# Sum of squares of the context tokens in the first norm: sixteen one-column matmuls into one PSUM bank in place of seven GpSimd additions and two matmuls

## The chip, the cores and the metric

One NeuronCore of a Trainium2 chip runs the whole program in one launch. The metric is device time in microseconds (us), the median over runs. The five engines have queues of their own and meet at semaphores: TensorE (PE in the profile; its weight loads are PEld), VectorE (DVE), ScalarE (ACT), GpSimd (POOL) and SyncE (SP, which here issues nearly all transfers).

## The reference, cut to what matters

A trunk of two layers over 512 latent and 256 context tokens, 1024 features, all in fp32. Each layer normalises the tokens, modulates them, projects them, mixes and attends, and ends in a squared-ReLU MLP. Context tokens go through the same weights with a modulation of their own. The change is in the first `rmsnorm` of layer 0, for the context tokens alone.

```python
def rmsnorm(x, g):
    xf = x.astype(jnp.float32)
    y = xf * lax.rsqrt(jnp.mean(xf * xf, axis=-1, keepdims=True) + EPS)
    return (y * g.astype(jnp.float32)).astype(x.dtype)
...
for l in range(DEPTH):                               # DEPTH = 2
    m_lat = modulation(c, w_mod[l], b_mod[l])        # silu(c) @ w_mod + b_mod: shifts, scales, gates
    m_ctx = modulation(c_ctx, w_mod[l], b_mod[l])
    h_lat = rmsnorm(x_lat, norm1_g[l]) * (1 + sc1) + sh1
    h_ctx = rmsnorm(x_ctx, norm1_g[l]) * (1 + csc1) + csh1
    z_lat, z_ctx = h_lat @ w_in[l], h_ctx @ w_in[l]  # q, k, v, u, gate
    # QK norm, rotary, attention (latents see context and latents), gated spatial mixing
    x_lat = x_lat + ga1 * (jnp.concatenate([attn_lat, gm_lat], -1) @ w_out[l])
    x_lat = x_lat + ga2 * sqrelu_mlp(modulate(rmsnorm(x_lat, norm2_g[l]), sh2, sc2), w_ff1[l], w_ff2[l])
    # the same for x_ctx in layer 0
return x_lat
```

## The kernel before

**Layout.** The stream lies transposed on the chip, features on the 128 partitions and tokens along the row. It is held in four tiles `X`, each with two blocks of 128 features by 768 tokens (512 latent, then 256 context), so there are KT = 8 feature blocks. Weights and activations are split in a rounded part `hi` and a remainder `lo`, and each product is three matmuls (hi·hi, hi·lo, lo·hi, line L203). ScalarE makes `hi` and VectorE makes `lo` (L207 and L208 for weights, L482 and L477 for normalised tokens, whose tiles are called `A`).

**The norm.** Class `Norm` does it in four steps. `step(k)` squares block k on ScalarE (L439, L442) and adds it to one tile `acc` (L444): on GpSimd for the context norm `cx`, on VectorE for the latent norm `lat`. `sums()` multiplies each 128 tokens of `acc` by a column of ones on TensorE (L453), which leaves a sum for each token on its own partition. VectorE then scales it (L456), takes the reciprocal root in nine small operations (L287 to L297) and spreads it on a diagonal, `w` (L466). `bcast()` turns that diagonal into a row on all partitions by one more matmul (L470, into a `pt` bank), and `apply()` multiplies and adds, block by block: L481 on VectorE into a tile `s`, L482 on ScalarE, L477 on VectorE.

**Shared buffers.** The squares (L442, `tsm`) and the products of `apply` (L481) come from one pool of three buffers, tag `s`. PSUM has two pairs of banks `pa`, two banks `pb`, two banks `pt`.

**The start.** `start()` is where the change lies. It loads and multiplies the modulation weights (`mod_chunk`, L338 and L351, into `pb` and `pt`), finishes the latent norm, and interleaves the first projection `kv0` (keys and values, `wide`, into two tiles `pa`). In between it places the context norm: `cx.step` for the eight blocks (`PAR['CL']` is 0), then `lat.apply` of blocks 4 to 7, then `cx.sums()` (`PAR["CS"]` is 0), then `kv0.wide` of blocks 4 and 5. After `start()` come `cx.bcast()`, `cx.apply`, the rest of `wide` and layer 0 itself: `u_part` (columns of `u`, into `pb`), `kv.bank(2)` (keys and values of the context tokens, into `pt`), and so on.

**What sets the order.** Inside `start()` TensorE and VectorE are under a manual schedule, and the framework's scheduler orders the rest; each engine then works through its queue strictly in that order. All transfers are issued by SyncE, whose order is the same in both kernels.

Of the kernel before, what the change touches and what calls it, by code (L numbers as in the profile page):

```python
# [11 lines left out]
AF = mybir.ActivationFunctionType  # L12
ALU = mybir.AluOpType
AX = mybir.AxisListType

D = 1024
KT = 8
# [5 lines left out]
EPS = 1e-6  # L23
# [137 lines left out]
def trunk(ctx: ExitStack, tc: tile.TileContext, xT, pk1, pk2, rope, wsT, w_mod, w_tok, w_u, w_out, w_ff1, w_ff2, outT):  # L161
    nc = tc.nc
    vec, act, pe, pool_e = nc.vector, nc.scalar, nc.tensor, nc.gpsimd
# [10 lines left out]
    def nm(s):  # L174
        seq[0] += 1
        return f"{s}_{seq[0]}"

    def unit(tag, shape, dt=F32R):
        return units.tile(shape, dt, tag=tag, name=nm(tag))
# [4 lines left out]
    def tsm(shape, dt=F32):  # L184
        return tmp.tile(shape, dt, tag="s", name=nm("s"), bufs=3)
# [4 lines left out]
    def small(n, dt=F32, tag="m", bufs=9):  # L190
        return tmp.tile([128, n], dt, tag=tag, name=nm(tag), bufs=bufs)
# [7 lines left out]
    def pt(shape=(128, 512)):  # L199
        return psum.tile(list(shape), F32, tag="t", name=nm("pt"), bufs=2)  # L200

    def mm(out, a, b, start, stop, n):
        pe.matmul(out, a, b, start=start, stop=stop)  # L203
        fl.vt += max(n / 2.4, 113.0) + 3.0
# [14 lines left out]
    def convert():  # L219

        if held:
            split(*held.pop(0))
# [57 lines left out]
    def rsqrt(v, n, l=0):  # L280

        if l:
            y = small(n)
            pool_e.tensor_tensor(out=y, in0=v, in1=mhalf[:, 0:n], op=ALU.pow)
            return y
        yi = small(n, I32)
        vec.tensor_scalar(yi, v.bitcast(I32), -0.5, 1595932665.0, op0=ALU.mult, op1=ALU.add)  # L287
        y = yi.bitcast(F32)
        t, r = small(n), small(n)
        vec.tensor_tensor(out=t, in0=y, in1=y, op=ALU.mult)  # L290
        vec.scalar_tensor_tensor(out=t, in0=t, scalar=-0.703952253, in1=v, op0=ALU.mult, op1=ALU.mult)
        vec.scalar_tensor_tensor(out=y, in0=t, scalar=1.681914091, in1=y, op0=ALU.add, op1=ALU.mult)
        vec.tensor_tensor(out=t, in0=y, in1=y, op=ALU.mult)
        vec.tensor_tensor(out=r, in0=t, in1=v, op=ALU.mult)
        vec.tensor_scalar(t, r, 0.375, -1.25, op0=ALU.mult, op1=ALU.add)
        vec.tensor_tensor(out=t, in0=t, in1=r, op=ALU.mult)
        vec.scalar_tensor_tensor(out=y, in0=t, scalar=1.875, in1=y, op0=ALU.add, op1=ALU.mult)  # L297
        return y
# [6 lines left out]
    ones = const.tile([128, 128], F32, name="ones")  # L305
# [3 lines left out]
    X = [unit(f"X{i}", [128, 2, T], F32) for i in range(4)]  # L309
# [17 lines left out]
    def mod_chunk(l, j, lag=1200.0):  # L327


        ps = pb()  # L330
        ns = PAR["NS"] if j < 4 else 4
        rows = ns * 32
        for kb in range(0, 4, ns // 2):
            ws_ = take("mod", l, j, kb)[:ns // 2]
            for k2 in range(ns):
                k = kb * 2 + k2
                q = k2 * 32
                pe.matmul(ps[q:q + 32, :], S32[:, k, :], ws_[k2 // 2][:, k2 % 2 * 512:(k2 % 2 + 1) * 512], start=k < ns, stop=k >= KT - ns)  # L338
            fl.vt += PAR["MV"] * ns
            if j > 3:  # L340
                release()
            if kb < 4 - ns // 2:
                yield

        tr = (tw if l == 0 and j < 4 else tsm)([128, 512])
        vec.transpose(tr[0:rows], ps[0:rows])

        def fin():
            p4 = pt((128, 4, 2))
            for a in range(4):  # L350
                pe.matmul(p4[a * 32:a * 32 + 32], P1("sel")[0:rows], tr[0:rows].rearrange("p (m a i) -> p a m i", m=4, a=4)[:, a, :, 0:2], start=True, stop=True)  # L351
            mod_store(l, j, p4)
        if lag:
            fl.defer(lag, fin)
        else:
            fin()
        yield
# [56 lines left out]
    cx = kv0 = None  # L414
# [8 lines left out]
    def run(gen):  # L423
        for _ in gen:
            fl.tick()


    class Norm:
        def __init__(self, l, w, off, n, cond):
            self.l, self.w, self.off, self.n, self.cond = l, w, off, n, cond  # L430
            self.acc = None
            self.tagn = 1 << (2 * l + w)

        def step(self, k):
            off, n = self.off, self.n
            if k == 0:
                tg = "acc0" if off == 0 else "acc1"
                self.acc = tmp.tile([128, n], F32, tag=tg, name=nm(tg), bufs=1)
                act.activation(self.acc, xk(0)[:, off:off + n], AF.Square)  # L439
                return  # L440
            sq = (tw if self is cx and PAR['SQ'] else tsm)([128, n])
            act.activation(sq, xk(k)[:, off:off + n], AF.Square)  # L442
            eng = pool_e if k < 7 and PAR["NP"] & self.tagn or self is cx else vec
            eng.tensor_tensor(out=self.acc, in0=self.acc, in1=sq, op=ALU.add)  # L444
# [624 lines left out]
    def start():  # L1069
        nonlocal held  # L1070
        for k in range(KT):
            lat.step(k)
        run(mod_chunk(0, 0, PAR["S0"]))
        lat.sums()
        run(mod_chunk(0, 2, PAR["S2"]))
        convert()
        lat.bcast()
        fl.tick(PAR["S2"])
        lat.apply(h0, range(4))
        kv0.passes(0)  # L1080
        run(mod_chunk(0, 1, PAR["S1"]))
        for k in range(KT if PAR['CL'] == 0 else 0):
            cx.step(k)
        g = mod_chunk(0, 3, 1.0)
        for k in range(4):
            next(g)
            if k == 3:
                convert()
            kv0.wide([k])
            fl.tick()  # L1090
        fl.tick(1.0)
        lat.apply(h0, range(4, KT), lambda k: convert() if k == 6 else None)
        for k in range(KT if PAR['CL'] == 1 else 0):
            cx.step(k)
        if PAR["CS"] == 0:
            cx.sums()
        kv0.wide(range(4, PAR["KB"]))
        if PAR["CS"] == 1:
            cx.sums()
# [4 lines left out]
    lat, cx = Norm(0, 0, 0, 512, 0), Norm(0, 0, 512, 256, 1)  # L1104
# [4 lines left out]
    if PAR["MS"]:  # L1109
        with tc.manual_schedule(engines=MSS[PAR["MS"]]):  # L1110
            start()
    else:
        start()
# [65 lines left out]
```

## Time and profile before

| | |
|---|---|
| median of 3 runs | 1510.93 us (1507.56 to 1514.46) |
| profiled execution | 1510.43 us, span in the trace 1508.6 us |
| busy over the span | PE 97%, PEld 85%, DVE 60%, ACT 42%, POOL 23% |
| mean granted clock of TensorE | 0.994 of full speed |
| L444 additions on POOL, in the start | 7, from 37.46 us on for 6.43 us |
| L453 for the context | 4 passes from 43.95 us on |

In the rows below, times are microseconds from the span's start. A row of the timeline has the start, the time it takes, the engine, the line, the operation, the tile it writes, an arrow and the tiles it reads, the shape, and the number merged; in square brackets stands how long the engine was idle before it and what ended that. On TensorE a row's duration includes the way through the array, so the pace of a series is read from starts. A row of the stretches has its bounds and length, then for PE, PEld, DVE, ACT and POOL the busy time and, in brackets, the instructions, then the granted clock of TensorE (1 is full), the share of the transfer engines that is busy, and GB/s.

### The profile page before, as it was taken

Reading aid. Unit: us, or ns where it says so; the run is one execution under the profiler, and the core shown is the slowest. Engines: PE = TensorE matmul, PEld = TensorE weight load, DVE = VectorE, ACT = ScalarE, POOL = GpSimd, SP = SyncE. Lnnn points to the kernel's source line nnn. Section 1 sums busy time; section 2 is a strip of 40 time slices with the busy share of each in tenths; the row PEclk is TensorE's granted clock in tenths of the full one; section 3 lists DMA queues with packets and bytes.
Section 4 is the critical chain, followed back from the end, with each engine's and each line's share of the span. In section 5 each row is a group of like instructions: output and inputs, shape, how many; then the busy total and the mean of one; then the engine's idle time right before and its main releaser. Section 6 shows DMA issues by size and latency. Waiting matters only on the chain.

```text
span 1508.6 us, 22398 instructions
## 1 busy us (share of the span) xinstructions
PE 1461.8 (97%) x8804; PEld 1289.5 (85%) x8804; DVE 908.6 (60%) x1667; ACT 641.0 (42%) x1078; POOL 342.1 (23%) x322
## 2 busy tenths in 40 slices
PE   6899899999999999999999999999999999999998
PEld 2899787797889899898989888997898888888887
DVE  5877967786755555444444537766887544444443
ACT  3543355674545353433333224536774333322221
POOL 0112421312145552322323213146222000000000
PEclk9999999999999999999999999999999999999999
DMA  9221344401133334333433211221001333333232
GB/s 363 65 71 57 112 176 162 140 1 43 60 112 126 114 124 126 103 122 111 126 112 126 98 56 57 88 81 57 29 1 56 113 98 98 98 98 98 98 95 73
DMA packets 49945, 148.80 MB, mean 99 GB/s; under 512 B 5424, under 2 KB 6832, under 8 KB 49840
## 3 DMA queue, kind: packets, MB, share of 16 engines
q1 hardware_dynamic: 49264, 146.46, 29.6%
q8 instruction: 69, 1.13, 0.3%
q10 hardware_dynamic: 576, 0.92, 0.2%
q14 instruction: 36, 0.29, 0.1%
HBM read 145.26 MB, written 2.10 MB: 98 GB/s over the span
## 4 chain that ended last, share of the span: by engine, by line
PE 83%; DVE 8%; ACT 3%; DMA 2%; POOL 2%; issue 2%; SPq 0%; POOLq 0%; ACTq 0%; DVEq 0%
PE pa L203 52%; PE pb L203 23%; PE pt L860 3%; PE pt L203 2%; PE pb L338 1%; POOL acc L444 1%; DMA raw<-in_w_tok 1%; DMA B<-in_w_mod 1%; PE pt L642 1%; DMA A<-in_w_mod 1%; DVE A L863 1%; DVE m L841 1%; DVE B L977 1%; ACT w L844 1%; PE pb L881 0%
## 5 line engine op out<-in xcount | busy, mean ns | idle before, releaser
L203 PE MATMUL pa<-A,hi 128*128 128x384 f32 (+2 forms) x1696 | 450.5, 348 | 1.9 <-ACT w L970 0.6
L207 ACT CAST hi<-raw 128x1024 fp32r<-128x1024 f32 x171 | 179.6, 1051 | 478.2 <-PE pa L203 378.1
L208 DVE TENSOR_TENSOR lo<-raw,hi 128x1024 fp32r<-128x1024 f32 x155 | 196.9, 1270 | 230.7 <-ACT hi L207 227.3
L203 PEld LDWEIGHTS pa<-A,hi 128*128 128x128 f32 x1696 | 305.5, 189 | 26.5 <-ACT w L970 1.8
L203 PE MATMUL pa<-A,lo 128*128 128x384 f32 (+2 forms) x848 | 294.1, 347 | 1.0 <-DVE lo L208 1.0
L203 PE MATMUL pa<-B,hi 128*128 128x512 f32 (+1 forms) x900 | 239.8, 355 | 3.6 <-DVE X L800 3.6
L382 POOL TENSOR_TENSOR C<-C,s 128x512 f32<-128x512 f32 x112 | 164.9, 1489 | 314.6 <-ACT s L381 272.6
L203 PEld LDWEIGHTS pa<-B,hi 128*128 128x128 f32 x900 | 158.8, 189 | 31.6 <-DVE X L800 5.9
L203 PEld LDWEIGHTS pa<-A,lo 128*128 128x128 f32 x848 | 159.8, 189 | 12.4 <-DVE lo L208 1.5
L800 DVE SCALAR_TENSOR_TENSOR X<-pa,modT,X 128x512 f32<-128x512 f32 x126 | 82.9, 660 | 140.9 <-PE pa L203 140.9
L203 PE MATMUL pb<-B,hi 128*128 128x512 f32 (+1 forms) x600 | 156.9, 350 | 0.9 <-DVE X L800 0.9
L203 PE MATMUL pa<-B,lo 128*128 128x512 f32 (+1 forms) x450 | 157.7, 355 | 0.0
L203 PE MATMUL pb<-hi,A 128*128 128x256 f32 x672 | 126.2, 285 | 0.0
L800 DVE SCALAR_TENSOR_TENSOR X<-pb,modT,X 128x512 f32<-128x512 f32 (+3 forms) x116 | 70.8, 618 | 81.8 <-PE pb L203 81.6
L203 PEld LDWEIGHTS pb<-B,hi 128*128 128x128 f32 x600 | 104.3, 189 | 16.0 <-DVE X L800 2.6
L203 PEld LDWEIGHTS pb<-hi,A 128*128 128x128 f32 x672 | 106.1, 191 | 0.3 <-PE pb L203 0.2
L203 PE MATMUL pb<-B,lo 128*128 128x512 f32 (+1 forms) x300 | 104.5, 348 | 0.0
L203 PE MATMUL pb<-lo,A 128*128 128x256 f32 x336 | 95.3, 284 | 0.0
L203 PEld LDWEIGHTS pa<-B,lo 128*128 128x128 f32 x450 | 84.1, 189 | 11.4
L381 ACT ACTIVATE s<-k,silu 128x512 f32<-128x512 f32 x112 | 76.9, 715 | 38.8 <-DMA k<-in_w_mod 25.9
L203 PE MATMUL pb<-A,hi 128*128 128x512 f32 (+2 forms) x288 | 81.7, 360 | 2.4 <-POOL A L791 2.4
L844 ACT ACTIVATE w<-pa,m 128x768 f32<-128x768 f32 (+1 forms) x80 | 65.6, 820 | 33.7 <-DVE m L841 25.2
(173 smaller groups left out, 2234.6 us busy)
## 6 DMA issues: line engine op xcount, KB each, us to landing
raw<-in_w_ff SPq DMA_DIRECT2D x128, 512.0 KB, 3.5
k<-in_w_mod SPq DMA_DIRECT2D x96, 256.0 KB, 3.0
raw<-in_w_tok SPq DMA_DIRECT2D x19, 512.0 KB, 3.4
raw<-in_w_out SPq DMA_DIRECT2D x16, 512.0 KB, 3.5
lo<-in_w_mod SPq DMA_DIRECT2D x16, 512.0 KB, 4.5
hi<-in_w_mod SPq DMA_DIRECT2D x16, 512.0 KB, 3.7
A<-in_w_mod SPq DMA_DIRECT2D x8, 512.0 KB, 9.7
raw<-in_w_u SPq DMA_DIRECT2D x8, 512.0 KB, 3.5
```

The source lines that it names most:

```text
L203: pe.matmul(out, a, b, start=start, stop=stop)
L207: act.copy(hi, src)
L208: (eng or vec).tensor_tensor(out=lo, in0=src, in1=hi.bitcast(F32), op=ALU.subtract)
L338: pe.matmul(ps[q:q + 32, :], S32[:, k, :], ws_[k2 // 2][:, k2 % 2 * 512:(k2 % 2 + 1) * 512], start=k < ns, stop=k >= KT - ns)
L381: act.activation(p, w, AF.Copy, scale=s)
L382: pool_e.tensor_tensor(out=a, in0=a, in1=p, op=ALU.add)
L444: eng.tensor_tensor(out=self.acc, in0=self.acc, in1=sq, op=ALU.add)
L642: pe.transpose(p[:, o:o + 128], stk[:, t, hh, c0:c0 + 128].bitcast(F32), ident)
L800: vec.scalar_tensor_tensor(out=xs, in0=src[:, s - off:e - off], scalar=modT[l][:, i * 8 + m, cond:cond + 1], in1=xs, op0=ALU.mult, op1=ALU ...
L841: vec.tensor_reduce(out=nmx, in_=ps[:, 0:nk], axis=AX.X, op=ALU.max, negate=True)
L844: act.activation(p, ps[:, 0:nk], AF.Exp, bias=nmx, accum_out=sm)
L860: pe.transpose(tp_[:, (kt - k0) * 128:(kt - k0) * 128 + 128], p[:, kt * 128:kt * 128 + 128], ident)
```

## The change

The eight `cx.step` calls go. In place of `cx.sums()` stands `cx.quick()`: ScalarE squares two feature blocks at once (256 tokens each, so 512 elements a partition), four times, and TensorE multiplies every 128 tokens of every block by the column of ones, all added in two columns of one `pt` bank. GpSimd has no part in it any more. The squares now stand behind `lat.apply`, ahead of `kv0.wide` of blocks 4 and 5.

```diff
+        def quick(self):
+            ps = pt()
+            nt = self.n // 128
+            for i in range(4):
+                sq = tsm([128, 2, self.n])
+                act.activation(sq, X[i][:, :, self.off:self.off + self.n], AF.Square)
+                for t in range(nt):
+                    for a in range(2):
+                        pe.matmul(ps[:, t:t + 1], sq[:, a, t * 128:(t + 1) * 128], ones[:, 0:1], start=i == 0 and t == 0 and a == 0, stop=i == 3 and t == nt - 1 and a == 1, skip_group_check=True)
+            v = small(nt)
+            vec.tensor_scalar(v, ps[:, 0:nt], 1.0 / D, EPS, op0=ALU.mult, op1=ALU.add)
+            self.diag(rsqrt(v, nt, self.l))
...
         run(mod_chunk(0, 1, PAR["S1"]))
-        for k in range(KT if PAR['CL'] == 0 else 0):
-            cx.step(k)
         g = mod_chunk(0, 3, 1.0)
...
         lat.apply(h0, range(4, KT), lambda k: convert() if k == 6 else None)
-        for k in range(KT if PAR['CL'] == 1 else 0):
-            cx.step(k)
         if PAR["CS"] == 0:
-            cx.sums()
+            cx.quick()
         kv0.wide(range(4, PAR["KB"]))
```

Three places show how the order moves. In the changed kernel the lines between the first hunk and `start()` are 14 higher, and the sums are L443.

**TensorE, behind the last modulation matmuls (L351).** `pt_408` is the bank of the sums, `pa_317` that of the projection `kv0`. Before:

```order
L351 MATMUL pt_383<-w_367,c_70 32x8 x4
L453 MATMUL pt_408<-ones,acc_74_291 128x1 x2
L203 MATMUL pa_317<-hi_134,A_43_175 128x256
L203 MATMUL pa_317<-lo_135,A_43_175 128x256
L203 MATMUL pa_317<-hi_134,A_43_175 128x256 x2
```

Now, with `pb_568` and `pb_598` the banks of two parts of `u`, whose weights are `hi_142`, `lo_143` and `hi_146`:

```order
L351 MATMUL pt_360<-w_344,c_70 32x8 x4
L203 MATMUL pb_568<-A_39_171,hi_142 128x512 x2
L203 MATMUL pb_598<-A_39_171,hi_146 128x512 x2
L203 MATMUL pb_568<-A_39_171,lo_143 128x512
L203 MATMUL pb_568<-A_40_172,hi_142 128x512 x2
L443 MATMUL pt_385<-ones,s_386 128x1 x4
L203 MATMUL pb_568<-A_40_172,lo_143 128x512
L203 MATMUL pb_568<-A_41_173,hi_142 128x512 x2
L203 MATMUL pb_568<-A_41_173,lo_143 128x512
L203 MATMUL pb_568<-A_42_174,hi_142 128x512 x2
L443 MATMUL pt_385<-ones,s_392 128x1 x4
L203 MATMUL pb_568<-A_42_174,lo_143 128x512
```

Seven matmuls of `u` stood behind the sums and now stand ahead of the first group of them; the third and the fourth group follow the last row shown, each behind two more matmuls of `u`, and then come the 24 matmuls of `kv0` on blocks 4 and 5.

**ScalarE, at the squares.** `A_43` to `A_46` are the `hi` parts of the latent blocks 4 to 7, `hi_142` and `hi_146` the casts of the two `u` weights. Before:

```order
L442 ACTIVATE s_305<-X_3_78 128x256
L442 ACTIVATE s_308<-X_4_79 128x256
L442 ACTIVATE s_311<-X_4_79 128x256
L482 ACTIVATE A_43_175<-s_390,modT_90 128x512
L207 CAST hi_142<-raw_140 128x1024
L482 ACTIVATE A_44_176<-s_393,modT_90 128x512
L207 CAST hi_146<-raw_144 128x1024
L482 ACTIVATE A_45_177<-s_397,modT_90 128x512
L482 ACTIVATE A_46_178<-s_403,modT_90 128x512
L207 CAST ws_165<-raw_163 128x512
```

Now:

```order
L496 ACTIVATE A_43_175<-s_367,modT_90 128x512
L207 CAST hi_142<-raw_140 128x1024
L496 ACTIVATE A_44_176<-s_370,modT_90 128x512
L207 CAST hi_146<-raw_144 128x1024
L496 ACTIVATE A_45_177<-s_374,modT_90 128x512
L440 ACTIVATE s_386<-X_1_76 128x512
L496 ACTIVATE A_46_178<-s_380,modT_90 128x512
L440 ACTIVATE s_392<-X_2_77 128x512
L440 ACTIVATE s_398<-X_3_78 128x512
L440 ACTIVATE s_404<-X_4_79 128x512
L207 CAST ws_165<-raw_163 128x512
```

The squares moved from ahead of the four `A` rows to between and behind them. In the built program `s_392` takes the buffer of `s_386`, and `s_404` that of `s_392`, so each of these two squares waits for the TensorE group that reads the buffer.

**TensorE, at the projection of the context tokens.** `pt_667` (now `pt_666`) is the bank of `kv.bank(2)`, `pb_637` (now `pb_636`) that of the context part of the first `u`. Before, the last of 42 matmuls into the one, and then the other:

```order
L203 MATMUL pt_667<-hi_134,A_43_175 128x256
L203 MATMUL pt_667<-hi_134,A_44_176 128x256
L203 MATMUL pt_667<-lo_135,A_44_176 128x256
L203 MATMUL pt_667<-hi_134,A_44_176 128x256
L203 MATMUL pb_637<-A_39_171,hi_142 128x256 x2
```

Now, the last of 25:

```order
L203 MATMUL pt_666<-lo_135,A_46_178 128x256
L203 MATMUL pt_666<-hi_134,A_46_178 128x256
L203 MATMUL pt_666<-hi_114,A_39_171 128x256
L203 MATMUL pb_636<-A_39_171,hi_142 128x256 x2
L203 MATMUL pb_636<-A_39_171,lo_143 128x256
```

Seventeen matmuls of that bank went behind the `u` part. Some 30 rows further on the two orders of TensorE run alike again (into `pb_768`, now `pb_767`, its second half of tokens), and from there to the end nothing differs on any engine.

## The prediction

> **What bounds the kernel.** I read the busy shares first, then who waited for whom on TensorE, then stretches of the start, then its timeline.
>
> ```profile
> PE 1461.8 (97%) x8804; PEld 1289.5 (85%) x8804; DVE 908.6 (60%) x1667; ACT 641.0 (42%) x1078; POOL 342.1 (23%) x322
> ...
> PE pb L338 <- DVE w L621: 5.6, 1, 5.6
> PE pt L453 <- POOL acc L444: 4.0, 1, 4.0
> ```
>
> TensorE is the bound. GpSimd's additions cost it one wait of 4.0 us, at the place of the change. The stretches split there (the third ends where the bank of `kv.bank(2)` begins, the fourth where the two orders become alike):
>
> ```profile
> 39.98:43.95 3.97, 0.01 (x2) 0.00 (x1) 2.23 (x6) 1.64 (x4) 3.60 (x5) 0.89 0.40 132
> 43.95:49.89 5.94, 5.94 (x27) 5.84 (x28) 5.79 (x8) 3.76 (x5) 0.00 (x0) 0.50 0.19 44
> 49.89:64.31 14.42, 14.42 (x78) 12.43 (x77) 10.90 (x35) 5.43 (x12) 0.00 (x0) 1.00 0.24 74
> ...
> 43.00:43.20 0.20, 0.00 (x0) 0.00 (x0) 0.14 (x2) 0.06 (x1) 0.12 (x2) 0.66 0.18 62
> 43.20:43.60 0.40, 0.00 (x0) 0.00 (x0) 0.40 (x1) 0.40 (x1) 0.40 (x1) 0.50 0.00 0
> ...
> 180.00:182.00 2.00, 0.76 (x8) 0.00 (x0) 2.00 (x1) 1.60 (x3) 2.00 (x2) 1.00 0.78 260
> 182.00:183.00 1.00, 0.00 (x0) 0.00 (x0) 1.00 (x2) 0.00 (x0) 1.00 (x1) 1.00 0.92 377
> 183.00:184.00 1.00, 0.00 (x0) 0.00 (x0) 1.00 (x1) 0.00 (x0) 1.00 (x1) 0.51 0.32 127
> ```
>
> The wait cost more than itself: the granted clock fell to 0.50 at 43.06 (a mean of 0.66 over 43.00 to 43.20) and stayed there until 49.89, though TensorE worked without a gap from 43.95 on. All that could be won here is the wait and half of the 5.94 us, 6.9 us.
>
> **The change on TensorE's path.** The rows that price it, from the timeline:
>
> ```profile
> 17.66 1.05 PE L453 MATMUL pt<-ones,acc 128*128 128x1 f32 x8
> 17.66 0.97 PEld L453 LDWEIGHTS pt<-ones,acc 128*128 128x128 f32 x8 [0.84 <-issue]
> 39.74 0.24 PE L351 MATMUL pt<-w,c 64*32 64x8 f32 x8
> 43.95 1.01 PE L453 MATMUL pt<-ones,acc 128*128 128x1 f32 x4 [3.96 <-POOL acc L444]
> 44.82 0.56 PE L203 MATMUL pa<-hi,A 128*128 128x256 f32 x1
> 47.96 0.63 PE L203 MATMUL pb<-A,hi 128*128 128x512 f32 x1
> 48.38 0.63 PE L203 MATMUL pa<-hi,A 128*128 128x256 f32 x2
> 55.91 0.60 PE L470 MATMUL pt<-w,ones 128*128 128x256 f32 x2
> 56.15 0.58 PE L203 MATMUL pb<-A,hi 128*128 128x512 f32 x1
> 64.31 0.28 PE L203 MATMUL pt<-hi,A 128*128 128x256 f32 x1
> 69.34 0.40 PE L203 MATMUL pb<-A,hi 128*128 128x256 f32 x2
> 78.04 0.36 PE L203 MATMUL pb<-hi,A 128*128 128x256 f32 x1
> ```
>
> The two sums of 256 tokens are four passes, so the sixteen are 32. A pass costs its weight load: 0.97 / 8 = 0.12 us at full clock, (44.82 − 43.95) / 4 = 0.22 at half. A matmul of 512 columns takes 48.38 − 47.96 = 0.42 us at half clock and (64.31 − 56.15) / 35 = 0.23 at full; one of 256 takes (69.34 − 64.31) / 42 = 0.12.
>
> When each group can start is set by ScalarE and VectorE:
>
> ```profile
> 7.60 0.61 ACT L442 ACTIVATE s<-X 128x512 f32<-128x512 f32 x1
> 43.14 0.72 ACT L482 ACTIVATE A<-s,modT 128x512 fp32r<-128x512 f32 x1 [1.22 <-DVE s L481]
> 43.77 1.03 ACT L207 CAST hi<-raw 128x1024 fp32r<-128x1024 f32 x1
> 44.71 0.72 ACT L482 ACTIVATE A<-s,modT 128x512 fp32r<-128x512 f32 x1
> ...
> 40.26 0.45 DVE L411 SCALAR_TENSOR_TENSOR A<-modT,c 128x8 f32<-128x8 f32 x1
> 42.31 1.56 DVE L481 SCALAR_TENSOR_TENSOR s<-X,A,pt 128x512 f32<-128x512 f32 x2 [1.61 <-POOL acc L444]
> 43.90 0.75 DVE L477 SCALAR_TENSOR_TENSOR A<-s,modT,A 128x512 fp32r<-128x512 f32 x1
> 44.57 0.74 DVE L481 SCALAR_TENSOR_TENSOR s<-X,A,pt 128x512 f32<-128x512 f32 x1
> 46.13 1.22 DVE L208 TENSOR_TENSOR lo<-raw,hi 128x1024 fp32r<-128x1024 f32 x1
> 50.38 0.15 DVE L456 TENSOR_SCALAR m<-pt 128x2 f32<-128x2 f32 x1
> 50.82 0.69 DVE L208 TENSOR_TENSOR ws<-raw,ws 128x512 fp32r<-128x512 f32 x1 [0.29 <-ACT ws L207]
> 53.20 0.43 DVE L466 TENSOR_TENSOR w<-c,m 128x256 f32<-128x256 f32 x1
> 56.54 0.87 DVE L481 SCALAR_TENSOR_TENSOR s<-X,A,pt 128x256 f32<-128x256 f32 x2 [2.92 <-PE pt L470]
> 67.61 0.67 DVE L696 SCALAR_TENSOR_TENSOR C<-s,pb 128x512 f32<-128x512 f32 x1
> ```
>
> *Removed.* GpSimd held `apply` too: its product L481 waited 1.61 us for a buffer `s`. It now starts at 40.71, when L411 ends, and ScalarE follows at 41.5 (product 0.74). The queue there is unchanged up to the second cast, so `hi_142` ends at 43.2 (0.63 from one start to the next, then 1.03) and, behind `A_44`, `hi_146` at 44.75 (its weights have landed: nothing moves from 43.20 to 43.60, by the last column above, and no transfer changes its place). GpSimd's seven additions and ScalarE's eight squares fall away beside other work.
>
> *The first wait that is left.* TensorE is done with L351 at 39.98 and now waits for `hi_142`: 43.22 − 39.98 = 3.24 us where it was 3.97. Two matmuls (0.85 at half clock), then 0.73 until `hi_146` at 44.80, two more, then 0.14 for `lo_143`. VectorE makes that from 44.5 on, behind two products and two `lo` parts, and needs 1.22. Three more matmuls end at 47.07.
>
> *The groups.* `s_386` follows `A_45` on ScalarE and is ready at 45.9, so no wait. Its eight passes at half clock take 1.74 us, to 48.8. Then `s_392` may be written (0.61, to 49.6), while six matmuls of `u` run: at half clock until 49.89, if the clock keeps its times, then at full, to 50.70. The second group ends at 51.67, two matmuls at 52.13, the third group at 53.1; `s_404`, which could start at 51.8, is there at 52.4. The cast of `ws` moves behind it and ends at 53.0, ahead of VectorE's L208 on it, which stands behind L456. Two matmuls and the fourth group end at 54.53. The exchange between the two engines is thus covered, by 1.1 us in each case; without that cover each of two squares would cost up to 0.6.
>
> *Behind the groups.* `kv0` on blocks 4 and 5 (24 matmuls, 2.88 us) ends at 57.4. VectorE's chain takes 53.63 − 50.38 − 0.29 = 2.96 us from L456 to the diagonal, so the diagonal comes at 57.6. Before, it was done long ahead of L470 (53.63 against 55.91). Now TensorE waits 0.25 us for it. L470 (0.24), 24 matmuls for blocks 6 and 7, 9 and 22 of 512 for `u` (7.2) lead to the `kv.bank(2)` matmuls at 68.0, which began at 64.31 before. Twenty-five of them (3.0) lead to `pb_636` at 71.0. Its bank must be free: L696 ended at 68.28 in a chain that L470 started and that was dense from 56.54 on; L470 comes 1.75 later, so it ends at 70.0, a second before it is needed. From there 78.04 − 69.34 = 8.70 us, and seventeen matmuls (2.04), to the point where the orders meet: 81.75 against 78.04.
>
> **The sum**, by TensorE's time up to that point: waits 3.24 + 0.73 + 0.14 + 0.25 − 3.97 = +0.4; passes 1.74 + 24 × 0.12 − 0.87 = +3.8; half clock −0.5 (4.1 us of matmuls at half instead of 5.07, half of each lost). Together **+3.7 us**. Beyond that point the engines work in the same order, and the delay reaches the end, as these rows say:
>
> ```profile
> 120.00:130.00 10.00, 10.00 (x86) 10.00 (x86) 5.67 (x24) 1.84 (x4) 1.67 (x2) 1.00 0.06 22
> 130.00:180.00 50.00, 49.59 (x417) 47.95 (x419) 46.03 (x139) 19.39 (x32) 15.94 (x12) 1.00 0.25 86
> ```
>
> TensorE is full there and VectorE idle for 4.3 of 10 us, waiting for matmuls.
>
> The unknown cost is a pass placed between long matmuls. The nearest rows have them in a row. Were its load wholly hidden behind the matmul ahead, the passes would cost nothing and the sum would be about 0; were each to take the half-clock price throughout, 28 × 0.22 gives +6.2 for that term and some 6 in all. I take 0.12, since eight in a row at full clock is just what a group is. Against the profiled execution of 1510.43 us the sum gives 1514.1; the median of the runs shown lies 0.5 above that execution, so 1514.6.
>
> **Rivals.** *The clock stays at full speed* (0.2). The Trainium skill, "TensorE: Matmul & The Clock Gate", section "What's actually happening", has the clock return to half after at least one idle window of about 3.4 us. By that the wait of 3.24 us would leave it at full. The trace speaks against a full window of idleness as the condition: here the clock fell at 183.0 and at 43.06 after less.
>
> By the rows, at 183.0 it fell after some 2.2 us without a matmul (0.76 us of work in 180 to 182), at 43.06 after 3.1. A wait of 3.24 us lies near enough to both that it may or may not. If it doesn't fall, the groups end at 52.66 and L470 starts at 55.8 instead of 57.65: 1.9 less, so +1.8 us, 1512.7.
>
> *The clock stays at half through the groups* (0.12, the side of slower). It stayed at half in 43.06 to 46.5 with TensorE busy for 2.5 of 3.4 us, so it wants more than that; if passes of one column don't count as work, every stretch with a group in it falls short until the last is through. Then the second group ends at 53.1 and the fourth at 58.3, L470 starts at 62.0 instead of 57.65, 4.3 later: +8.0 us, 1518.9. It decides from the point where the clock still reads 0.50 at 56; one stretch more alone gives +5.3.
>
> *The delay is absorbed* (0.08). At 186 TensorE waits 5.6 us for VectorE (L621, above). If VectorE's queue there came from work that doesn't follow TensorE, that wait would swallow all: 1510.9. Its idle time at 120 to 130 speaks against it.
>
> **How the numbers follow.** My path has 0.55, the three rivals 0.4, and 0.05 is left for what I don't see, spread to both sides. The runs of before differ by 6.9 us, so 0.5% (7.6 us) is about what can be told from no change. The range reaches from the absorbed delay, less a microsecond of that spread, to the slow clock: 1510 to 1519.5. Only the slow clock and the spread above my path reach 1518.5: slower 0.13. Faster by 0.5% would need more than the 6.9 us that could be won, at no cost: 0.04. Same: 0.83.
>
> **What would show it.** Right: TensorE idle from about 40 to 43.2 with ScalarE's cast as releaser, a gap of 0.7 behind two matmuls, L443 32 passes of about 1 us a group, the `kv.bank(2)` matmuls from 68, no wait longer than 0.5 us between 47 and 82, and no L444 on POOL before the first stack. Wrong: a wait at the second or fourth group (the exchange of the buffer isn't covered), at the diagonal or at `pb_636` of over a microsecond, or a clock that is not at half from 43 to 50.

## The result, and the profile after

The changed kernel is slower: 1520.55 us (median of 6 runs, 1516.19 to 1524.67) against 1510.01 us (6 runs, 1507.56 to 1514.46), a ratio of 1.0069 with a 95% interval of 1.0056 to 1.0083. That is +10.5 us where +3.7 was forecast, and it lies above the range. The profiled execution took 1523.29 us.

The page's spans and busy shares, and below them who TensorE waited for:

```profile
span 1521.5 us, 22439 instructions
...
PE 1474.5 (97%) x8832; PEld 1299.9 (85%) x8832; DVE 909.7 (60%) x1667; ACT 640.3 (42%) x1074; POOL 335.9 (22%) x315
...
PE pb L338 <- DMA A<-in_w_mod: 13.0, 2, 12.6
PE pb L338 <- DVE w L635: 7.9, 1, 7.9
...
PE pb L203 <- ACT hi L207: 3.5, 2, 3.0
```

The wait for GpSimd (4.0 us before) is gone, and 3.5 us of waiting for ScalarE's casts stand in its place. PE is busy for 12.7 us more in a span that is 12.9 us longer: almost nothing of the loss is idle time. The timeline of TensorE at the change, with the first row of each step:

```profile
43.16 1.22 PE L203 MATMUL pb<-A,hi 128*128 128x512 f32 x2 [3.01 <-ACT hi L207]
44.84 1.22 PE L203 MATMUL pb<-A,hi 128*128 128x512 f32 x2 [0.46 <-ACT hi L207]
...
47.15 1.70 PE L443 MATMUL pt<-ones,s 128*128 128x1 f32 x8
...
51.41 1.70 PE L443 MATMUL pt<-ones,s 128*128 128x1 f32 x8
...
53.97 1.70 PE L443 MATMUL pt<-ones,s 128*128 128x1 f32 x8
...
56.53 1.70 PE L443 MATMUL pt<-ones,s 128*128 128x1 f32 x8
...
63.12 0.59 PE L484 MATMUL pt<-w,ones 128*128 128x256 f32 x2
...
73.48 0.28 PE L203 MATMUL pt<-hi,A 128*128 128x256 f32 x1
...
87.39 0.40 PE L203 MATMUL pb<-hi,A 128*128 128x256 f32 x2
```

All four groups take the same 1.70 us, and none waits. L484 (the former L470) starts at 63.12, 5.5 us later than forecast; the matmuls of `kv.bank(2)` at 73.48; the point where the two orders meet is at 87.39, against 78.04 before: **+9.35 us** by then. Why all groups are equally slow, the stretches say (bounds and length, then busy time of PE, PEld, DVE, ACT, POOL, then the granted clock):

```profile
42.30:45.70 3.40, 2.08 (x4) 1.00 (x4) 3.25 (x5) 3.39 (x5) 0.00 (x0) 0.50 0.21 84
45.70:49.10 3.40, 3.40 (x13) 3.11 (x13) 3.06 (x4) 1.12 (x3) 0.00 (x0) 0.50 0.28 77
49.10:52.50 3.40, 3.40 (x12) 2.82 (x12) 0.00 (x0) 0.98 (x2) 0.00 (x0) 0.50 0.48 154
52.50:55.90 3.40, 3.40 (x14) 3.21 (x15) 0.00 (x0) 1.14 (x2) 0.00 (x0) 0.50 0.00 0
55.90:59.30 3.40, 3.40 (x15) 3.21 (x15) 0.99 (x4) 0.00 (x0) 0.00 (x0) 0.50 0.02 5
59.30:62.80 3.50, 3.50 (x18) 3.50 (x18) 1.57 (x9) 0.00 (x0) 0.00 (x0) 0.50 0.45 150
```

The clock fell at 42.30, about where forecast, but it came back at 62.78 and not at about 50: 20.5 us at half instead of the 6.8 before. From 45.7 on TensorE is "busy" for 3.40 of every 3.40 us. The second to the fifth stretch hold one-column passes; the first one that is full of work without any (59.30 to 62.80) is followed by full clock. It is not this one execution alone: the mean granted clock of the six runs was 0.987 to 0.994, and that of the kernel before, in the comparisons with the experiments, 0.993 to 0.997. The theory was thus (1) that one-column passes don't count as work for the clock. Against it stood (2) that any row of passes shorter than their weight load does this, whatever their width, and (3) that the clock is beside the point and a pass between matmuls is simply dearer, or that the place of the groups behind a wait matters.

### The profile page after: what moved, and what is told of

It is laid out like the page before. It is cut to its first block, busy times and chain, and to the rows that moved or that the text cites. A ratio compares the mean times of both kernels' runs of the same rounds, so it can differ in the third digit from the quotient of the medians.

```text
span 1521.5 us, 22439 instructions
## 1 busy us (share of the span) xinstructions
PE 1474.5 (97%) x8832; PEld 1299.9 (85%) x8832; DVE 909.7 (60%) x1667; ACT 640.3 (42%) x1074; POOL 335.9 (22%) x315
## 4 chain that ended last, share of the span: by engine, by line
PE 84%; DVE 8%; ACT 3%; POOL 2%; issue 2%; DMA 1%; SPq 0%; POOLq 0%; ACTq 0%; DVEq 0%
PE pa L203 52%; PE pb L203 23%; PE pt L874 3%; PE pt L203 2%; PE pb L338 2%; DMA A<-in_w_mod 1%; PE pt L656 1%; DVE A L877 1%; ACT hi L207 1%; DVE B L991 1%; ACT w L858 0%; DVE lo L208 0%; DVE m L855 0%; PE pb L895 0%; POOL acc L458 0%
```

## The experiments

How each compares is gathered here. The clock is the mean granted one in the stretch from 40 to 64 us of one profiled execution, and 2 x 24 x (1 - clock) are the microseconds at half. The last column runs from the start of the last modulation matmuls (L351, at about 39.7) to the start of TensorE's wait ahead of L338 (at about 181), which takes out that TensorE comes to L351 at times up to 1.4 us apart; before: 186.34 - 5.58 - 39.74. In the comparisons with the experiments, the kernel before had medians of 1509.3 to 1509.7 us.

| kernel | median us (runs) | ratio to before, 95% interval | clock 40 to 64 | L351 to wait |
|---|---|---|---|---|
| before | 1510.01 (6) | | 0.86 | 141.0 |
| changed | 1520.55 (6) | 1.0069, 1.0056 to 1.0083 | 0.57 | 150.2 |
| changed, again | 1518.83 (1) | | 0.64 | 149.7 |
| e1 128 columns | 1512.43 (11) | 1.0021, 1.0012 to 1.0030 | 0.86 | 144.7 |
| e2 behind kv0 | 1513.64 (5) | 1.0032, 1.0019 to 1.0044 | 0.79 | 144.7 |
| e9 both of these | 1512.06 (11) | 1.0020, 1.0012 to 1.0029 | 1.00 | 140.7 |
| e3 before, sums behind kv0 | 1509.96 (11) | 1.0003, 0.9994 to 1.0011 | 0.86 | 140.8 |
| e4 ones as weights | 1513.59 (6) | 1.0029, 1.0017 to 1.0040 | 0.93 | 143.0 |
| e6 e4 behind kv0 | 1511.17 (11) | 1.0010, 1.0001 to 1.0019 | 0.86 | 142.7 |
| e8 e6, rounded squares | 1510.97 (12) | 1.0005, 0.9995 to 1.0014 | 0.93 | 140.4 |

**The columns alone (e1).**

```diff
-pe.matmul(ps[:, t:t + 1], sq[...], ones[:, 0:1], ...)
+pe.matmul(ps[:, t * 128:(t + 1) * 128], sq[...], ones, ...)
```

> The changed kernel with the all-ones matrix whole as the moving operand: each of the 32 passes now streams 128 columns instead of one into the same bank; weights, squares and the number of passes are the same (groups two to four stand nearer together, before kv0's blocks 4 and 5). Theory 1 (passes of one column don't count as TensorE's work for the clock, so that the clock stayed at half from 42.3 to 62.8 until a stretch of 3.4 us without them): the stretches with groups are now full of work, the clock is back at full at about 49 (two stretches of 3.41 as before the change, three at most: 52.5), the groups behind it cost 0.12 us a pass, and the point where TensorE's orders meet comes at about 81 to 83 (before 78.04, changed 87.39); 1512 to 1516 us. Rival 2 (any row of short passes, whose weight load is longer than their streaming, holds the clock, however many columns they have): half until the last group is through, 59 or later, orders meet at 86 or later, 1518 to 1521. Rival 3 (the clock had nothing to do with it and a pass between matmuls is simply dearer): 0.19 us a pass whatever the clock, about 1518.

Measured: 1512.43 us, and the clock back at full at 50.49, after two stretches. The stretches of this kernel, the last of them with most of the 24 passes that stand in a row:

```profile
43.50:47.00 3.50, 2.70 (x7) 1.57 (x7) 3.35 (x6) 3.07 (x5) 0.00 (x0) 0.52 0.08 15
47.00:50.30 3.30, 3.30 (x14) 3.02 (x14) 1.84 (x3) 1.79 (x4) 0.00 (x0) 0.50 0.45 136
50.30:53.80 3.50, 3.50 (x31) 3.44 (x31) 1.25 (x5) 0.68 (x2) 0.00 (x0) 0.97 0.65 224
...
49.78 3.33 PE L443 MATMUL pt<-ones,s 128*128 128x128 f32 x24
52.86 0.36 PE L203 MATMUL pa<-hi,A 128*128 128x256 f32 x1
```

The passes are as many and their weights the same; each now streams 128 columns for one, and yet the kernel is 8 us faster. Of the 24 passes from 49.78 on, the first four start at half clock, about 0.2 us apart; the other twenty, from 50.57 on, take (52.86 - 50.57) / 20 = 0.11 us each, close to the 0.12 of the forecast. Rival 3's dearer pass falls, and so does rival 2, since the clock opens while such passes run and stays open on them. One reservation: the scheduler also moved groups two to four together, so the place isn't quite the same. With its clock as before the change, e1 stands 3.7 us behind the kernel before in the last column: about what the forecast's passes and waits come to by themselves.

**The place alone (e2), and both (e9).**

```diff
-            cx.quick()
         kv0.wide(range(4, PAR["KB"]))
+        cx.quick()
```

> The changed kernel with the one-column sums moved behind kv0's blocks 4 and 5 (24 dense matmuls), so that kv0 comes first after the wait at 40 us and the groups stand among kv0's block 6 and u. Theory 1: the first full stretch of dense matmuls after the wait reopens the clock, so full at about 50 or 53, before the first group. Then either a stretch with one group (about 1 of 3.4 us) is work enough to keep a clock that is at full: the groups cost 0.12 a pass, the orders meet at about 81 to 83, 1512 to 1515 us; or it falls short at full clock too: the clock falls again among the groups and 1517 to 1521. Rivals 2 and 3 give the same as in the changed kernel, a clock at half while groups run or 0.19 us a pass at any clock: 1518 to 1521.

> Both one-variable edits together: 128 columns instead of one, behind kv0's blocks 4 and 5. With e1 and e2 it makes the square of columns by place. Theory 1: one to two stretches of half clock from the wait at 40 and none behind it (e2's second fall at 52.7, two stretches, is gone: 3.4 us won against e2, e2's wait for L338 began at 184.0, so about 180.6 to 182). If the second fall in e2 came from its place (the work standing round it) and not from the columns, it comes again here and the wait begins at 184. About 1510 to 1512 us.

In e2, `kv0` brought the clock back at 45.8 and then it was lost again, without a gap in TensorE's work (bounds and length, PE busy, granted clock; the first three rows all instructions, the last two the one-column passes alone):

```profile
45.80:49.20 3.40, 3.40 (x27) 1.00 0.46 105
49.20:52.60 3.40, 3.40 (x32) 1.00 0.35 131
52.70:56.00 3.30, 3.30 (x16) 0.50 0.20 35
...
49.20:52.60 3.40, 2.24 (x20) 1.00 0.35 131
52.70:56.00 3.30, 0.89 (x5) 0.50 0.20 35
```

The stretch with 2.24 us of one-column passes costs the clock: it is at half behind it, for two stretches. So the passes do not only fail to open the clock; they close it on an engine that never idles. In e9, with 128 columns at that place, there is no such fall. The mean from 40 to 64 is 1.00 by the table, so the wait of 2.1 us at 40 didn't cost the clock either, where one to two stretches had been expected. The wait for L338 began at 186.22 - 5.58 = 180.6, where theory 1 had 180.6 to 182 and its rival 184.

Between e2 and e9 lie 4.0 us in the last column of the table, and not all of that is the columns: e2 also spent a first stretch at half (42.41 to 45.82, before any of the passes), which cost it half of 3.4 us, while e9 escaped this after the same wait. The second fall, two full stretches, cost half of 6.8. In the medians the distance is 1.6. The other four runs of e2 have mean clocks of 0.993 to 0.994, the profiled one 0.993, so they probably lost it too; why they are up to 3.2 us faster than the profiled one isn't shown. Nor does e9 keep its lead: its last column ties with the kernel before, its median is 2.4 above. Behind the wait for L338 its trace has 11.9 us of work at half clock in three places and the trace before 6.7, and half of that difference is 2.6.

**The cost by itself (e5, e10).** In the kernel before, where TensorE is full of 512-column matmuls at full clock, rows of 40 extra matmuls are put in, which the trace shows as 80 passes:

```diff
+        def ladder(c):
+            ps = pt()
+            for j in range(40):
+                pe.matmul(ps[:, 0:c], ident if j % 2 else ones, ones[:, 0:c], start=j == 0, stop=j == 39)
...
+            if l == 1 and m in LADDER:        # e5: 1, 16, 32, 64, 96, 128 columns; e10: 128, 56, 48, 40, 32, 1
+                ladder(LADDER[m])
```

> The kernel before, with six rows of extra passes put into the second layer's feed-forward stage, where TensorE is full of 512-column matmuls at full clock from 1180 to 1500 us and waits for nobody: 80 passes in a row each (the first row broken once), with 1, 16, 32, 64, 96 and 128 columns, their weights ready, their result unused. Theory 1 (what counts for the clock is columns streamed, not instructions or loads): during the row of one column the clock falls to half within two stretches of 3.41 us although TensorE never idles, and with 128 columns it doesn't (24 such passes in a row left it at full behind the wait); it says nothing of where between the two the limit lies. A pass costs 0.12 us at full clock whatever its columns. Rival 2 (rows of passes bound by their weight load): it falls in all six. Rival 3 (the clock follows idle time alone): it falls in none, the six rows cost 480 x 0.12 = 58 us in all and nothing more.

> The ladder of extra passes once more, in the other direction and finer: rows of 80 passes with 128, 56, 48, 40, 32 and 1 columns, the narrow ones now last, at 1425 us and later. In the first ladder the clock fell in the rows of 1, 16 and 32 columns and not in those of 64, 96 and 128; but these came later too. Theory 1 (columns streamed): none with 128, half clock in the rows of 32 and 1 (5 stretches between them by the first ladder's 2 and 3), and the rows of 56, 48 and 40 show where between 32 and 64 the limit lies. If the place was what counted, the early rows fall and the late ones don't.

The stretches from each row's first pass to its last, in the order of the expectation, first of e5 and then of e10 (bounds and length, PE busy, granted clock):

```profile
1215.90:1224.30 8.40, 8.40 (x65) 0.82 0.19 64
1269.80:1284.10 14.30, 14.30 (x81) 0.60 0.12 38
1324.90:1336.60 11.70, 11.70 (x81) 0.74 0.15 46
1376.90:1385.60 8.70, 8.70 (x81) 1.00 0.19 62
1429.40:1438.10 8.70, 8.70 (x80) 1.00 0.23 62
1481.90:1490.60 8.70, 8.70 (x80) 1.00 0.21 63
```

```profile
1217.30:1226.10 8.80, 8.80 (x79) 1.00 0.22 63
1269.80:1278.60 8.80, 8.80 (x81) 1.00 0.22 61
1317.80:1329.60 11.80, 11.80 (x73) 0.65 0.14 46
1370.80:1382.20 11.40, 11.40 (x78) 0.73 0.16 47
1427.80:1442.10 14.30, 14.30 (x81) 0.60 0.12 38
1488.40:1501.90 13.50, 13.50 (x81) 0.63 0.12 41
```

PE is busy throughout all twelve. The clock stays full for 56, 64, 96 and 128 columns and falls for 1, 16, 32, 40 and 48 (48 and 56 by one row each); whether a row comes early or late makes no difference. Only the number of stretches was a miss: the row of 32 lost three in e5 and five in e10, that of one column (broken in e5, as expected there) two and four. Where it stays full, a pass takes 8.7 / 80 = 0.11 us, whatever its width. Rivals 2 and 3 of e5 (all fall, none falls) are both refuted. e5 as a whole took 1578.58 us, 69 more than before: 480 passes of 0.11 are 53, and half of the three falls' 6.8 + 17.0 + 10.2 us of half clock are 17.

**Where the wait of 4.0 us at 40 comes from (e3).** In the kernel before, the four passes of the sums are moved behind `kv0`'s blocks 4 and 5:

```diff
-PAR = {... "CS": 0 ...}
+PAR = {... "CS": 1 ...}
```

> The kernel before, GpSimd's additions and all, with only its four passes that sum over partitions moved behind kv0's blocks 4 and 5, so that TensorE no longer waits for GpSimd ahead of kv0. If the wait of 3.97 us at 40 was GpSimd's alone, it is gone and 1506 us. If kv0's own operands (the second h at 43.9 to 44.7, the cast weights at 43.2 to 44.7) stand right behind it, as the changed kernel showed (3.01 and 0.46 us with GpSimd out of the way), less than 1 us is won: 1509 to 1511, with the wait put down to ScalarE's cast. All theories of the clock agree here: half for two stretches, as before.

1509.96 us, no change, and the wait is of the same length with another releaser:

```profile
PE pa L203 <- ACT A L482: 3.9, 1, 3.9
```

So the sums' own wait for GpSimd is worth nothing: the next operand, ScalarE's `A`, is just as late. That doesn't clear GpSimd, though. Its additions are still in this kernel, and they hold `A` back by way of the buffers `s`, as they did before. From e3, and below it from e9, where they are gone and `kv0` stands first as well:

```profile
41.59 1.55 DVE L481 SCALAR_TENSOR_TENSOR s<-X,A,pt 128x512 f32<-128x512 f32 x2 [1.61 <-POOL acc L444]
```

```profile
42.27 0.39 PE L203 MATMUL pa<-hi,A 128*128 128x256 f32 x1 [2.08 <-ACT A L496]
```

Without the additions the wait is 2.1 us and not 3.9. What the change takes off GpSimd is thus worth 1.8 us of waiting, and it gives more than that back for 28 further passes of 0.10 to 0.12 us.

**The operands swapped (e4), behind kv0 (e6), and with rounded squares (e8).** With the ones as weights, the 256 squares stream, the sums come out on all partitions, and the diagonal and its matmul fall away; the root is done on 128x256. e8 writes squares and ones in the rounded form of the other matmuls and so drops the squares' low bits.

```diff
-for t in range(nt):
-    for a in range(2):
-        pe.matmul(ps[:, t:t + 1], sq[:, a, t * 128:(t + 1) * 128], ones[:, 0:1], ...)
+for a in range(2):
+    pe.matmul(ps[:, 0:self.n], ones, sq[:, a, :], start=i == 0 and a == 0, stop=i == 3 and a == 1)
```

> The changed kernel's squares with the operands swapped: the ones are the weights and the squares stream, so that 16 passes of 256 columns give the sums on all partitions at once; the diagonal and L484's matmuls, which spread the root over the partitions, fall away, and VectorE does the root on 128x256 instead of 128x2 (ten steps of about 0.4 us instead of 0.15: about 4 us instead of 3). Theory 1: no pass of one column is left, full clock at about 49, the passes cost 16 x 0.12 to 0.22 = 2 to 3.5 us for 0.9 that before's four took, L484's 0.24 is saved; orders meet at 79 to 82, 1511 to 1515 us. If something else than the columns held the clock (the waits between squares, the exchange of the buffer with ScalarE), it stays at half until 59 or later, and 1517 to 1520.

> The ones as weights and 256 columns streamed, behind kv0's blocks 4 and 5: both edits in one kernel. From the two runs apart: the first wait 2.1 us instead of 4.0 (-1.6, with 0.3 for the second product), one stretch of half clock instead of two (-1.7), sixteen passes of 0.12 for four (+1.0 against 0.9 at half clock), no L470 matmul (-0.2): the wait for L338 begins some 2.5 us earlier than before, and 1506.5 to 1508.5 us. It would be no better than the kernel before (1510) if VectorE's root over 128x256, now later, makes kv0's blocks 6 and 7 or the first bank's reader wait.

> The kernel of both edits (ones as weights, 256 columns, behind kv0) with squares and ones written in the rounded 32-bit form that the other matmuls use, so that a matmul is one pass and not two; the squares lose their low bits. In the run with both edits a pass of 256 unrounded columns took 2.57 / 12 = 0.21 us, and not the 0.12 I had put down from the rounded matmuls of the same width. Eight passes of 0.12 are 1.0 instead of 3.4 us: 2.4 us won against that run, whose wait for L338 began at 181.5 (before 180.8): 179.1 here, and about 1508.5 us, 0.1% under the kernel before; with the longer wait for VectorE there (7.9 instead of 5.6 in that run's trace) 1511. If the rounded passes are no cheaper, 1511 as in that run.

The clock did what theory 1 says: one stretch at half in e4, two in e6, one in e8, and no fall among the passes (e4's first four ran at half, in the very stretch that brought the clock back). The gain did not come: e6 reached the wait for L338 1.6 us later than before by the table, where 2.5 earlier was expected, and it had one stretch of half clock more than I had counted on. That stretch is worth half of 3.4 us. The rest lies for the most part in the passes, which I had priced at 0.12 us from the rounded matmuls of that width. From e6's timeline, and below it e8's:

```profile
49.44 2.92 PE L442 MATMUL pt<-s,ones 128*128 128x256 f32 x12
52.01 0.47 PE L203 MATMUL pa<-hi,A 128*128 128x256 f32 x1
```

```profile
49.70 0.40 PE L443 MATMUL pt<-s,k 128*128 128x256 f32 x2
49.94 0.40 PE L203 MATMUL pa<-hi,A 128*128 128x256 f32 x2
...
72.61 0.66 PE L668 MATMUL pt<-c,k 128*128 128x128 f32 x4 [0.85 <-ACT B L669]
77.21 1.09 PE L668 MATMUL pt<-c,k 128*128 128x128 f32 x8 [0.94 <-POOL k L656]
```

An unrounded pass takes (52.01 - 49.44) / 12 = 0.21 us, a rounded one 0.24 / 2 = 0.12 and there are half as many. The dearer passes and the stretch make 1.5 + 1.7 = 3.2 of the 4.1 us by which e6 missed; the rest isn't accounted for.

e8 then won what was expected of it: 2.3 us against e6 in the last column, where 2.4 stood. Its wait for L338 began at 188.48 - 7.85 = 180.6 and not at the expected 179.1 mainly because TensorE came to L351 1.4 us later than in e6. The sum is partly luck: the passes won 2.4 and one stretch of half clock less some 1.6, and two new waits, 1.8 us for ScalarE and GpSimd at 72 and 77 in the last two rows, took about as much back as the clock had given. No version here beats the kernel before: e8 is the same as it within the interval, e3 too.

**The changed kernel once more (e7).**

> The changed kernel once more, unaltered, for a second trace. Theory 1: half clock from about 42 to about 59 to 63 again, five or six stretches, with TensorE full; the matmul where the orders meet at 86 to 88. What only one trace shows (7.9 us of wait for VectorE at 190 instead of 5.6, three stretches of half clock behind it instead of two) comes again if it follows from the later arrival there, and not if it was that execution's own; with it about 1522 us, without it about 1518.

1518.83 us. The last group and L484 again, and the mean clock over 17 us:

```profile
42.13 0.73 PE L203 MATMUL pb<-A,hi 128*128 128x512 f32 x2 [3.01 <-ACT hi L207]
...
55.51 1.70 PE L443 MATMUL pt<-ones,s 128*128 128x1 f32 x8
...
61.53 0.60 PE L484 MATMUL pt<-w,ones 128*128 128x256 f32 x2
...
42.20:59.20 17.00, 16.10 (x59) 0.54 0.14 47
```

The early loss comes again (149.7 in the table), with five stretches instead of six: the clock is at half from 43.43 to 60.50. The wait ahead of L338 was 5.58 us, and not 7.85: that part of the first trace was that execution's own.

## Why the prediction was wrong

- *What failed:* "at half clock until 49.89, if the clock keeps its times, then at full". I let the clock return two stretches after the fall, as before the change, and did not ask what TensorE does in those stretches. They held one-column passes, and so did each up to 59.3. By the forecast's prices the clock's share was -0.1 us: -0.5 for matmuls, +0.78 for the first group at half (1.74 - 8 x 0.12), -0.39 for the four old passes (0.87 - 4 x 0.12). Measured: some 19.2 us of work at half (20.5 less 1.3 idle), so 9.6 lost, less half of the 5.94 before: **+6.6**. To the point where the orders meet the forecast missed by 9.35 - 3.7 = 5.6; the clock missed by 6.7, and shorter waits gave 0.9 of it back.
- *Passes:* right. At full clock 32 x 0.12 less 4 x 0.12 is +3.4. Measured at full clock were 0.11 us in e1 and the ladders, and 0.10 in e2, whose groups of eight stand between matmuls (47.34 to 48.15 for one). So the load of a pass between matmuls is not hidden, which was the open point.
- *Waits:* right in place and kind, a little too long: 3.01 and 0.46 where 3.24, 0.73 and 0.14 stood; none at the diagonal, which was ready long before the late L484; none at `pb_636`. Less the 3.97: -0.5 instead of +0.4. The exchange of the squares' buffers was covered. The terms give 6.6 + 3.4 - 0.5 = 9.5 with 0.12 a pass and 8.9 with 0.10, about the measured 9.35.
- *"The delay reaches the end"*: right. At L338 both traces of the changed kernel are still 7.8 and 11.6 us late, the latter with the coincidence told of below.
- *The rivals:* "the clock stays at half through the groups" (0.12) was what happened, by the mechanism it named. Its own working had the second group end at 53.1 and the fourth at 58.3 (measured 52.97 and 58.09), but L484 at 62.0 instead of 63.12: the clock opens only after a further stretch of dense matmuls alone. So +9.35 instead of +8.0 there. The range ended just above this rival's 1518.9, so that one further stretch was enough to leave it. The evidence that the prediction gave for it, the stretch from 43.06 to 46.48 with four such passes and 2.5 of 3.4 us busy, did not show it: in e6 a stretch with 3.1 of 3.4 us busy and no such pass (40.93 to 44.35) did not open the clock either. It took the experiments to tell the two apart. The rival that the clock stays full fell; that the delay is absorbed at the wait for L338 fell as well.
- *From +9.35 to the end:* the two profiled executions differ by 12.9 us. 2.27 more are the longer wait ahead of L338. The clock's third stretch at half there costs only 0.6, since most of it is wait (4.75 us of work at half against 3.50 before), and a stretch at 356 that the trace before doesn't have costs 1.7. That makes 13.9, so 1.0 us comes back somewhere, and where isn't shown. Such stretches come and go at 190, 350, 1030 and 1160 us in these traces, some in one, some in another; that is as much as I know of why the runs of one kernel differ by several microseconds. The medians are 10.5 apart.

The Trainium skill, "TensorE: Matmul & The Clock Gate", section "What's actually happening", counts in free-running windows of about 3.4 us and has the clock back at full after a busy one and at half after an idle one. The window agrees: the half clock lasted 20.48 us, six times 3.413, and 17.07, five times, in the second trace. The trace differs on what a busy window is, since windows with TensorE busy for 3.40 of 3.40 us neither opened the clock (changed kernel) nor kept it (e2).

## What to carry to other kernels

A TensorE that reads as fully busy can still lose its clock, and a few one-column matmuls among dense ones can cost more by that than by their own time: read the granted clock beside the busy share, and add them up over each stretch of 3.4 us. Where a sum over partitions has to run on TensorE near a wait, let it stream more columns than it needs (56 or more held the clock here, and the pass was no dearer), or put it behind enough dense matmuls and few to a stretch (in e2 a stretch with one group of eight kept the clock, one with 20 passes lost it). Before taking an engine out of the way because a wait names it, move the waiting step alone, and if the next operand is just as late, follow what holds that one: here it was the same engine by way of a shared buffer, and the 1.8 us it held were fewer than what its work cost on TensorE.

## What the runs showed of the hardware

- *The limit lies between 48 and 56 columns a pass* of 0.11 us, with weights of 128x128. It doesn't look like a simple mean over the stretch: a 512-column matmul takes 0.23 us at full clock, so 56 columns stream for an estimated 0.025 of 0.11 us, 23%, and kept the clock; but 1.16 us of matmuls in the 3.41 before 183.01, 34%, did not. (Those are L338's, with weights of 32 columns instead of 128, so the two aren't quite alike.) What is counted stays open.
- *The same wait costs the clock or not, by where the stretches lie.* They run on through a trace: before, the falls at 43.06 and 183.01 are 41 times 3.413 us apart. TensorE waits the same 2.08 us at 40 in e2, e6, e8 and e9. The clock fell in the first three, at the end of a stretch with 1.06, 1.62 and 1.58 us of work; in e9, by stretches counted back from its next fall at 184.65, the wait lay across two, with 2.32 and 2.14 us of work, and the clock stayed. To come back it asked for more: a stretch with 3.14 of 3.41 us busy left it at half (e6), one with 3.37 brought it back (e4).
- *Some 10 ns decided 2.3 us.* Ahead of L338, VectorE's last small step starts together with GpSimd's L805 (L791 before). In the first trace of the changed kernel, and below it in the trace before:

```profile
186.55 1.84 DVE L297 SCALAR_TENSOR_TENSOR m<-m,m 128x8 f32<-128x8 f32 x1
...
186.54 3.61 POOL L805 TENSOR_TENSOR A<-C,A 128x768 fp32r<-128x768 f32 x2 [1.48 <-ACT A L804]
```

```profile
177.17 0.17 DVE L297 SCALAR_TENSOR_TENSOR m<-m,m 128x8 f32<-128x8 f32 x1
...
177.16 4.10 POOL L791 TENSOR_TENSOR A<-C,A 128x768 fp32r<-128x768 f32 x2 [1.48 <-ACT A L790]
```

  GpSimd starts 0.01 us ahead in both by these rows; by the nanoseconds in the traces it was 11 ahead in the changed kernel and 2 before. Where VectorE lost the race, a step of 0.17 us took 1.84, the next ones were late too, and TensorE waited 7.85 us instead of 5.58. It did so in three of the twelve traces (changed, e6, e8), those in which GpSimd was 7 to 11 ns ahead; in the other nine it was at most 4 ahead, or behind. The Trainium skill, "Trainium Architecture — The Big Picture", section "What this means for kernel authors", says that these two engines alone contend for a port and lock each other out; the 1.84 us agrees.
